# Last output projection: the final column group's weights loaded and split during the three groups ahead of it, and the residuals' loads re-timed

## The chip, the cores and the metric

One core of a Trainium2 chip. The time is device microseconds (us) of one execution of the whole program. Three runs of the kernel before give a median of 988.8 us (988.37 to 990.36).

## The reference, cut to what matters

Two layers of a decoder trunk on one sequence of 256 tokens, model width 2048, all float32. Each layer mixes the tokens (layer 0 a gated linear recurrence, layer 1 sparse attention), gates the result with `silu(z)`, projects it with a 2048 x 2048 matrix and normalises:

```python
h = x
for i in range(DEPTH):                       # DEPTH = 2
    y = mixer_i(h, ...)                      # ... @ w_out at its end
    h = _layer_norm(DEEPNORM_ALPHA * h + y, ln_g, ln_b)
return h
```

The change touches the end of layer 1 alone: `y = (o * silu(z)) @ l1_w_out`, the residual `alpha * h + y` (where `h` is layer 0's output) and the last layer norm.

## The kernel before, in words

**Arithmetic.** A float32 product is made from three matmuls: both operands are split into a high part (rounded by ScalarE, L82) and a low part (the rest, a subtraction on VectorE, L83). `split` (L80-83) does both. For a weight block the low part reads the block and its high part, so it runs after the high part; the block's raw buffer is free when the low part is done.

**The last projection.** `oT` (tiles named `b`, four of them, each four K tiles of 128) holds the gated attention output, transposed and split. The projection runs in four column groups of 512 (`for c in range(4)`, L980). A group's weights come in eight blocks, j = 0 to 7, of 256 rows by 512 columns (512 KB): `load` (L114) issues the DMA on SyncE's queue (SP), `parts` splits it. Groups 0, 1 and 2 use `project` (L173): block by block, both token tiles (t = 0, 1), two K tiles, three matmuls each (L166, L167, L168): 12 matmuls for a block. Blocks 6 and 7 of group 0 need the last tile of `b`, which the last head group of the attention writes at its end (`o` times `zT` on L906, then a split into `b`), first for t = 0, then for t = 1. The matmuls of the groups and those of the attention are interleaved on TensorE by the scheduler, and the order so made is fixed: every engine, and SP's queue, goes through its own list in order.

**Group 3** is done token tile by token tile (`project_by_tile`, L182), so that the layer norm of the first tile runs beside the second's matmuls. It needs all its eight blocks before its first tile ends. `summed` (L964) splits a block into its own tiles (`wh`, `wl` of the pool `late`, eight each) and also adds up the last 256 columns of the block (a reduction on VectorE, L972, and an accumulating copy on ScalarE, L973), from which the second tile's mean is had early.

**Buffers.** `slot` (L149) hands out raw buffers `wr` (three in this stage) and split buffers `wh` and `wl` (five each); whichever is free first is given. In the kernel before, the first three blocks of group 3 use `wr`, the other five are loaded into freed `wh` and `wl` buffers. The pool `late` is opened after group 1 is written down (L1035); its memory is that which the attention's pools (`kv`, `at`) held until `attention.close()`.

**Residuals.** For each group, `h` is rebuilt from layer 0's normalised rows: 512 KB of `norm0`, plus that group's 512 gains and 512 biases spread over the partitions (256 KB each), into a tile of `room`; then GpSimd (POOL) multiplies by the gain (L961, two instructions) and adds the bias (L962, two). When a residual's three loads are issued is written by hand: `turns` (L926) gives for each item n and step i the place (c, j), that is, behind block j of group c. `also` runs at each place, `other` does the step. Items 0 to 3 are the residuals of groups 0 to 3, item 4 the rows of the last norm's gain and bias. A residual with its projection's result gives a piece of `hb` and its statistics (L990, L992, VectorE). Residuals 0 and 2 share a tile of `room`, 1 and 3 another.

Of the kernel before, what the change touches and what calls it, by code (L numbers as in the profile page):

```python
# [8 lines left out]
F32 = mybir.dt.float32  # L9
# [8 lines left out]
D = 2048  # L18
S = 256
NT = S // 128  # L20
KT = D // 128
# [34 lines left out]
def trunk(ctx, tc, a, out):  # L56
# [54 lines left out]

    queued = [None]

    def load(w, j, c0, n, name="wr"):  # L114

        raw = (slot([128, 2, n], F32, name, 3, 1) if name == "wr" else
               slot([128, 1152], F32, name, 5, 3)[:, 0:2 * n].rearrange("p (k n) -> p k n", k=2))
        queued[0] = nc.sync.dma_start(raw, w[256 * j:256 * (j + 1), c0:c0 + n].rearrange(
            "(k p) n -> p k n", p=128)).ins
        return raw  # L120

    def weights(w, j, c0, n):
        return parts(load(w, j, c0, n))
# [55 lines left out]
                also(j)  # L179
        return ps  # L180

    def project_by_tile(xs, w, c0, after, behind=None, summed=None, also=None):  # L182

        ws = []
        for j in range(KT // 2):
            if summed:

                ws.append(summed(load(w, j, c0, 512, "wr" if j < 3 else ("wl", "wh")[j % 2])))
            else:
                hi, lo = weights(w, j, c0, 512)
                ws.append([(hi[:, kk], lo[:, kk]) for kk in range(2)])
            if also:
                also(j)

        def steps(ps, t, i, behind=None):
            for k in range(KT):
                hi, lo = ws[k // 2][k % 2][i:i + 2]  # L200
                with tc.issue_after(behind) if behind and k >= HOLD else nullcontext():
                    tok_step(ps, xs, k, t, hi, lo)
            return ps

        for t in range(NT):
            if summed and t == NT - 1:
                after(t, steps(pjb([128, 258]), t, 2), steps(pjb([128, 256]), t, 4))
            else:
                behind = after(t, steps(pjb([128, 512]), t, 0, behind))
        return behind  # L210
# [179 lines left out]
    with tc.tile_pool(name="start", bufs=4) as start:  # L390
# [3 lines left out]
        ps = mxb([128, 128])  # L394
# [504 lines left out]
    def gate(g, os):  # L899
# [9 lines left out]
        for t in range(NT):  # L909
# [13 lines left out]

    turns = [((0, 6), (0, 7), (0, 7)), ((1, 1), (1, 2), (1, 3)), ((1, 5), (1, 6), (1, 7)),  # L926
             ((2, 1), (2, 2), (2, 3)), ((3, 7), (3, 7), (3, 7), (3, 7))]
    turns = [(n, i, at) for n, v in enumerate(turns) for i, at in enumerate(v)]
    res = {}
    room = [acts.tile([128, 2, 2, 512], F32, name="room", tag="a") for _ in range(4)]  # L930
    rows = [room[i // 2][:, i % 2].rearrange("p u n -> p (u n)") for i in range(4)]
# [7 lines left out]
    def behind(o, src):  # L939
        with tc.issue_after(queued[0]):  # L940
            nc.sync.dma_start(o, src)

    def also(c, j):
        for n, i, at in turns:
            if at == (c, j):
                other(n, i)

    def other(n, i):
        if n == 4:
            i = 2 * (i % 2) + i // 2  # L950
            behind(rows[i], a[("l1_ln_g", "l1_ln_b")[i // 2]][None, D // 2 * (i % 2):D // 2 * (i % 2 + 1)]
                   .to_broadcast([128, D // 2]))
# [2 lines left out]
            behind(res[n][0], norm0[:, 512 * n:512 * (n + 1)].rearrange("(t p) d -> p t d", p=128))  # L955
        else:
            xr, gb = res[n]
            behind(gb[:, i - 1], a[("l0_ln_g", "l0_ln_b")[i - 1]][None, 512 * n:512 * (n + 1)]
                   .to_broadcast([128, 512]))
            for t in range(NT) if i == 2 else ():  # L960
                pool.tensor_tensor(xr[:, t], xr[:, t], gb[:, 0], op=OP.mult)  # L961
# [20 lines left out]
    for c in range(4):  # L982
# [22 lines left out]
        def finish(t, ps, other=None):  # L1005
# [13 lines left out]
            with tc.manual_schedule(engines={mybir.EngineType.DVE}):  # L1019
# [8 lines left out]
                centred(t, me[:, 5:6], (1536, known), (known, D))  # L1028
                scaled(t, mv[:, 3:4], (0, 256), (256, 512), *quarters[1:3], (1536, known), (known, D))

        if c < 3:
            for t, ps in enumerate(project(oT, a["l1_w_out"], 512 * c, lambda j, c=c: also(c, j))):
                residual(t, ps)
            if c == 1:
                late = ctx.enter_context(tc.tile_pool(name="late", bufs=8, side="right"))  # L1035
        else:
            project_by_tile(oT, a["l1_w_out"], 512 * c, finish, summed=summed, also=lambda j: also(3, j))


# [31 lines left out]
```

## Time and profile before

| | us |
|---|---|
| median of three runs | 988.8 |
| the profiled execution, its own time | 989.94 |
| its span, first to last instruction | 987.9 |
| TensorE busy (PE) | 972.9 |
| VectorE busy (DVE) | 695.9 |
| ScalarE busy (ACT) | 564.8 |
| GpSimd busy (POOL) | 111.0 |
| mean granted TensorE clock | 0.995 |

Rows of the profile's timeline give the start in us, the duration, the engine, the line, the operation, output and inputs by their tiles' names, shapes and a count; what stands in brackets is the idle time of the engine just before, and what ended it. `PE` is TensorE's matmuls, `SPq` SyncE's queue of DMA issues. Matmuls are pipelined: the time one costs is the distance to the next one's start, not its duration. A table of windows gives for each stretch the length, the busy time of each engine (with a count of instructions), the granted clock, the DMA engines' share and GB/s.

### The profile page before, as it was taken

What the parts mean: (1) busy time and instruction counts of PE and PEld (TensorE: products, weight loads), DVE (VectorE), ACT (ScalarE), POOL (GpSimd) and SP (SyncE); (2) the same over time, 40 slices, a digit from 0 to 9 for tenths busy, and PEclk for the clock granted to TensorE, in tenths of its full rate; (3) what the DMA queues carried; (4) which work ended last, traced back from release to release, by engine and by line L of the source; (5) the groups of instructions that cost most, each with busy time, mean ns of one, the idle gap of its engine ahead of it and who ended that gap; (6) DMA issues with size and microseconds to landing.
All of it is one profiled execution on the core that took longest, in us unless ns stands there. A gap on an engine that the chain in (4) does not pass through costs nothing.

```text
span 987.9 us, 14450 instructions
## 1 busy us (share of the span) xinstructions
PE 972.9 (98%) x5209; PEld 837.1 (85%) x5209; DVE 695.9 (70%) x1185; ACT 564.8 (57%) x940; POOL 111.0 (11%) x180
## 2 busy tenths in 40 slices
PE   9999999999999999999999999999999999999996
PEld 8888888888888888888888888988888888887885
DVE  6797678657865786656666755655767858797767
ACT  6754554464446544434476655565967747894450
POOL 1400200020002000310010020102001020004320
PEclk9999999999999999999999999999999999999998
DMA  9875565556555655457466776676454555156782
GB/s 306 263 230 176 176 173 168 171 160 192 171 171 161 190 167 171 163 182 259 154 232 209 259 235 207 179 207 182 135 162 138 169 163 140 56 169 213 250 295 94
DMA packets 126247, 185.16 MB, mean 187 GB/s; under 512 B 6224, under 2 KB 70816, under 8 KB 125920
## 3 DMA queue, kind: packets, MB, share of 16 engines
q1 hardware_dynamic: 123984, 177.89, 58.5%
q0 software_dynamic: 1472, 5.56, 1.9%
q8 instruction: 41, 0.67, 0.3%
q10 hardware_dynamic: 720, 0.79, 0.2%
q14 instruction: 30, 0.25, 0.1%
HBM read 180.02 MB, written 4.19 MB: 186 GB/s over the span
## 4 chain that ended last, share of the span: by engine, by line
PE 91%; ACT 3%; DVE 2%; issue 2%; DMA 2%; POOL 0%; SPq 0%; POOLq 0%; DVEq 0%; ACTq 0%
PE pjb L166 18%; PE pjb L168 18%; PE pjb L167 18%; PE pjb L230 13%; PE pjb L234 6%; PE pjb L224 4%; PE pjb L225 2%; PE mxb L506 2%; PE mxb L273 1%; PE mxb L641 1%; PE mxb L642 1%; PE mxb L643 1%; ACT p L848 1%; PE mxb L692 1%; PE mxb L691 1%
## 5 line engine op out<-in xcount | busy, mean ns | idle before, releaser
L83 DVE TENSOR_TENSOR wl<-wr,wh 128x1024 fp32r<-128x1024 f32 (+3 forms) x304 | 365.1, 1208 | 157.1 <-ACT wh L82 155.6
L82 ACT ACTIVATE wh<-wr 128x1024 fp32r<-128x1024 f32 (+3 forms) x304 | 312.1, 1033 | 276.9 <-PE pjb L168 142.8
L167 PE MATMUL pjb<-wl,a 128*128 128x512 f32 (+1 forms) x576 | 219.9, 382 | 0.0
L166 PE MATMUL pjb<-wh,a 128*128 128x512 f32 (+1 forms) x576 | 219.8, 382 | 0.0
L168 PE MATMUL pjb<-wh,a 128*128 128x512 f32 (+1 forms) x576 | 219.3, 381 | 0.0
L230 PE MATMUL pjb<-a,wh 128*128 128x512 f32 x544 | 141.5, 396 | 0.6 <-ACT wh L82 0.4
L168 PEld LDWEIGHTS pjb<-wh,a 128*128 128x128 f32 x576 | 108.4, 188 | 19.2
L166 PEld LDWEIGHTS pjb<-wh,a 128*128 128x128 f32 x576 | 108.2, 188 | 19.2
L167 PEld LDWEIGHTS pjb<-wl,a 128*128 128x128 f32 x576 | 108.3, 188 | 18.6
L230 PEld LDWEIGHTS pjb<-a,wh 128*128 128x128 f32 x544 | 97.3, 189 | 17.9 <-ACT wh L82 1.0
L166 PE MATMUL pjb<-wh,b 128*128 128x512 f32 (+2 forms) x272 | 103.5, 381 | 0.0
L168 PE MATMUL pjb<-wh,b 128*128 128x512 f32 (+2 forms) x272 | 103.5, 380 | 0.0
L167 PE MATMUL pjb<-wl,b 128*128 128x512 f32 (+2 forms) x272 | 103.3, 380 | 0.0
L224 PE MATMUL pjb<-a,wh 128*128 128x512 f32 x256 | 91.2, 396 | 0.0
L234 PEld LDWEIGHTS pjb<-a,wl 128*128 128x128 f32 x544 | 75.9, 188 | 6.3
L234 PE MATMUL pjb<-a,wl 128*128 128x256 f32 x544 | 79.5, 283 | 0.0
L225 PE MATMUL pjb<-a,wl 128*128 128x256 f32 x256 | 72.3, 283 | 0.0
L168 PEld LDWEIGHTS pjb<-wh,b 128*128 128x128 f32 x272 | 51.6, 190 | 9.7
L167 PEld LDWEIGHTS pjb<-wl,b 128*128 128x128 f32 x272 | 51.4, 189 | 9.5
L166 PEld LDWEIGHTS pjb<-wh,b 128*128 128x128 f32 x272 | 51.5, 189 | 9.4
L224 PEld LDWEIGHTS pjb<-a,wh 128*128 128x128 f32 x256 | 48.1, 188 | 10.2
L225 PEld LDWEIGHTS pjb<-a,wl 128*128 128x128 f32 x256 | 48.3, 189 | 0.4
(255 smaller groups left out, 1175.7 us busy)
## 6 DMA issues: line engine op xcount, KB each, us to landing
wr<-in_l_w_in_dram SPq DMA_DIRECT2D x216, 512.0 KB, 3.8
wr<-in_l_w_out_dram SPq DMA_DIRECT2D x59, 512.0 KB, 4.1
ws<-in_l_w_in_dram SPq DMA_DIRECT2D x12, 512.0 KB, 4.6
wr<-in_l_cmp_w_k_dram SPq DMA_DIRECT2D x5, 512.0 KB, 3.5
wr<-in_l_cmp_w_v_dram SPq DMA_DIRECT2D x5, 512.0 KB, 4.1
wr<-in_l_w_in_dram SPq DMA_DIRECT2D x9, 280.0 KB, 3.5
xr<-in_x_dram POOLq DMA_DIRECT2D x4, 512.0 KB, 5.8
norm<-hb POOLq DMA_DIRECT2D x2, 1024.0 KB, 5.6
```

Source lines behind the costliest of these rows:

```text
L82: act.activation(hi, src, AF.Copy)
L83: dve.tensor_tensor(lo, src, hi.bitcast(F32), op=OP.subtract)
L166: pe.matmul(ps, xh, wh, start=(k == 0), stop=False)
L167: pe.matmul(ps, xh, wl, start=False, stop=False)
L168: pe.matmul(ps, xl, wh, start=False, stop=(k == KT - 1))
L224: pe.matmul(ps[b], hi[:, 0, b], xs.both(k), start=(k == 0), stop=False, skip_group_check=True)
L225: pe.matmul(ps[b][:, S:2 * S], lo[:, 0, b], xs.at(k, slice(0, S))[0], start=False, stop=(k == KT - 1), skip_group_check=True)
L230: pe.matmul(o, hi[:, i, b], xs.both(k + i), start=(k + i == 0), stop=False, skip_group_check=True)
L234: pe.matmul(o[:, S:2 * S], lo[:, i, b], xs.at(k + i, slice(0, S))[0], start=False, stop=(k + i == KT - 1), skip_group_check=True)
L273: last[0] = pe.transpose(ps[:, i], src[:, i], ident).ins
L506: pe.matmul(ps[:, h], km[:, h].rearrange("p b r j -> p (b r j)"), later, start=True, stop=True)
L641: pe.matmul(o, a[0], b[0], start=start, stop=False)
```

## The change

Group 3's eight blocks are no longer loaded inside `project_by_tile`. They are item 5 of `turns`: behind certain blocks of groups 0, 1 and 2 `other` loads one, into a raw buffer `wr` like all the others, and hands it to `summed`; the results are kept in `ahead` and passed to `project_by_tile`. The pool `late` is opened ahead of group 0 instead of behind group 1. The loads of the residuals are re-timed; of the two rows of a residual the bias comes second and the gain last, and POOL's work follows the gain. Group 0's residual is written down in group 1, behind block 2 (`residuals(*done)` in `also`), the others as before behind their own group.

| item | before | after |
|---|---|---|
| residual 0 (norm0, then the two rows) | (0,6) (0,7) (0,7) | (0,2) (0,4) (1,0) |
| residual 1 | (1,1) (1,2) (1,3) | (0,6) (1,2) (1,4) |
| residual 2 | (1,5) (1,6) (1,7) | (1,7) (2,0) (2,1) |
| residual 3 | (2,1) (2,2) (2,3) | (2,6) (2,7) (2,7) |
| rows of the last norm | (3,7) | (2,7) |
| group 3's blocks 0 to 7 | in group 3 | (0,5) (0,7) (1,1) (1,3) (1,5) (1,7) (2,1) (2,3) |

```diff
-    def load(w, j, c0, n, name="wr"):
-        raw = (slot([128, 2, n], F32, name, 3, 1) if name == "wr" else
-               slot([128, 1152], F32, name, 5, 3)[:, 0:2 * n].rearrange("p (k n) -> p k n", k=2))
+    def load(w, j, c0, n):
+        raw = slot([128, 2, n], F32, "wr", 3, 1)
...
-    def project_by_tile(xs, w, c0, after, behind=None, summed=None, also=None):
-        ws = []
-        for j in range(KT // 2):
-            if summed:
-                ws.append(summed(load(w, j, c0, 512, "wr" if j < 3 else ("wl", "wh")[j % 2])))
...
+    def project_by_tile(xs, w, c0, after, behind=None, summed=None):
+        ws = summed or []
+        for j in range(KT // 2) if not summed else ():
+            hi, lo = weights(w, j, c0, 512)
...
+    late = ctx.enter_context(tc.tile_pool(name="late", bufs=8, side="right"))
...
+        if (c, j) == (1, 2):
+            residuals(*done)
     def other(n, i):
-        if n == 4:
+        if n == 5:
+            ahead.append(summed(load(a["l1_w_out"], i, D - 512, 512)))
+        elif n == 4:
...
-            behind(gb[:, i - 1], a[("l0_ln_g", "l0_ln_b")[i - 1]][None, 512 * n:512 * (n + 1)]
+            behind(gb[:, 2 - i], a[("l0_ln_b", "l0_ln_g")[i - 1]][None, 512 * n:512 * (n + 1)]
...
         if c < 3:
-            for t, ps in enumerate(project(oT, a["l1_w_out"], 512 * c, lambda j, c=c: also(c, j))):
-                residual(t, ps)
-            if c == 1:
-                late = ctx.enter_context(tc.tile_pool(name="late", bufs=8, side="right"))
+            done = residual, project(oT, a["l1_w_out"], 512 * c, lambda j, c=c: also(c, j))
+            if c:
+                residuals(*done)
         else:
-            project_by_tile(oT, a["l1_w_out"], 512 * c, finish, summed=summed, also=lambda j: also(3, j))
+            project_by_tile(oT, a["l1_w_out"], 512 * c, finish, summed=ahead)
```

In the order rows below a row is the line, the operation, output and inputs, and the shape; the number behind a tile's name tells its instances apart, and line numbers of the kernel after are seven lower to two higher than those of the same statement before.

**SyncE's queue, from the seventh load of group 0's weights.** Before:

```order
L118 DMA wr_8686<-in_l1_w_out_dram 128x2x512
L941 DMA room_8574<-norm0_76 128x2x512
L118 DMA wr_8705<-in_l1_w_out_dram 128x2x512
L941 DMA room_8574<-in_l0_ln_g_dram 128x512
L941 DMA room_8574<-in_l0_ln_b_dram 128x512
L118 DMA wr_8739<-in_l1_w_out_dram 128x2x512
L118 DMA wr_8757<-in_l1_w_out_dram 128x2x512
L941 DMA room_8575<-norm0_76 128x2x512
L118 DMA wr_8776<-in_l1_w_out_dram 128x2x512
```

After (`wr_8691`, `wr_8740` and `wr_8795` are group 3's blocks 0, 1 and 2; `wr_8703` and `wr_8722` blocks 6 and 7 of group 0; `wr_8754`, `wr_8777`, `wr_8807` and `wr_8834` blocks 0 to 3 of group 1):

```order
L117 DMA wr_8691<-in_l1_w_out_dram 128x2x512
L117 DMA wr_8703<-in_l1_w_out_dram 128x2x512
L938 DMA room_8578<-norm0_76 128x2x512
L117 DMA wr_8722<-in_l1_w_out_dram 128x2x512
L117 DMA wr_8740<-in_l1_w_out_dram 128x2x512
L117 DMA wr_8754<-in_l1_w_out_dram 128x2x512
L938 DMA room_8577<-in_l0_ln_g_dram 128x512
L117 DMA wr_8777<-in_l1_w_out_dram 128x2x512
L117 DMA wr_8795<-in_l1_w_out_dram 128x2x512
L117 DMA wr_8807<-in_l1_w_out_dram 128x2x512
L938 DMA room_8578<-in_l0_ln_b_dram 128x512
L117 DMA wr_8834<-in_l1_w_out_dram 128x2x512
```

Three blocks of group 3 stand among the loads of groups 0 and 1, and residual 0's gain now stands behind the first block of group 1. With three raw buffers, each load waits for the block three places ahead in its buffer: `wr_8691` and `wr_8807` share one, `wr_8740` and `wr_8834` the second, and `wr_8722`, `wr_8754`, `wr_8777`, `wr_8795` the third.

**VectorE, from the attention's last gating (`o` times `zT`) on.** Before:

```order
L83 TENSOR_TENSOR wl_8779<-wr_8776,wh_8778 128x1024
L906 TENSOR_TENSOR o_8163<-o_8163,zT_8455 128x256
L906 TENSOR_TENSOR o_8163<-o_8163,zT_8553 128x256
L83 TENSOR_TENSOR b_4571<-o_8163,b_4571 128x4x128
L990 SCALAR_TENSOR_TENSOR hb_8570<-room_8574,pjb_8576 128x256 x2
L992 BN_STATS stats_8571<-hb_8570 128x6 x2
L83 TENSOR_TENSOR wl_8798<-wr_8795,wh_8797 128x1024
L83 TENSOR_TENSOR wl_8821<-wr_8818,wh_8820 128x1024
```

After:

```order
L83 TENSOR_TENSOR wl_8780<-wr_8777,wh_8779 128x1024
L899 TENSOR_TENSOR o_8163<-o_8163,zT_8455 128x256
L899 TENSOR_TENSOR o_8163<-o_8163,zT_8553 128x256
L83 TENSOR_TENSOR b_4571<-o_8163,b_4571 128x4x128
L974 TENSOR_REDUCE ws_8695<-wr_8691 128x1
L974 TENSOR_REDUCE ws_8744<-wr_8740 128x1
L992 SCALAR_TENSOR_TENSOR hb_8570<-room_8577,pjb_8579 128x256 x2
L83 TENSOR_TENSOR wl_8694<-wr_8691,wh_8693 128x2x2x256
L994 BN_STATS stats_8571<-hb_8570 128x6 x2
L83 TENSOR_TENSOR wl_8743<-wr_8740,wh_8742 128x2x2x256
L83 TENSOR_TENSOR wl_8798<-wr_8795,wh_8797 128x2x2x256
```

Before, three blocks of group 1 are split ahead of the last gating (`wl_8779` is the third) and the fourth follows it; after, two are, and what follows the gating is the split of group 3's blocks 0, 1 and 2.

**TensorE, from the last matmuls of group 0's second token tile on.** Before:

```order
L166 MATMUL pjb_8577<-wh_8707,b_4571 128x512
L167 MATMUL pjb_8577<-wl_8708,b_4571 128x512
L168 MATMUL pjb_8577<-wh_8707,b_4571 128x512
L167 MATMUL pjb_8737<-wl_8779,b_4569 128x512
L168 MATMUL pjb_8737<-wh_8778,b_4569 128x512
L166 MATMUL pjb_8738<-wh_8778,b_4569 128x512
```

After:

```order
L165 MATMUL pjb_8580<-wh_8724,b_4571 128x512
L166 MATMUL pjb_8580<-wl_8725,b_4571 128x512
L167 MATMUL pjb_8580<-wh_8724,b_4571 128x512
L165 MATMUL pjb_8752<-wh_8809,b_4569 128x512
L165 MATMUL pjb_8753<-wh_8809,b_4569 128x512
L166 MATMUL pjb_8752<-wl_8810,b_4569 128x512
L167 MATMUL pjb_8752<-wh_8809,b_4569 128x512
```

Both go on to group 1's third block; before, its parts are `wh_8778` and `wl_8779`, after they are `wh_8809` and `wl_8810`, made from `wr_8807`.

## What was predicted ahead of the run

> **What bounds the kernel now.** I read the page first, then a table of windows over the last projection, then who TensorE waited for, then the timelines of TensorE, VectorE, ScalarE, GpSimd and the DMA queue around the one gap. The page's second line says who bounds:
>
> ```profile
> PE 972.9 (98%) x5209; PEld 837.1 (85%) x5209; DVE 695.9 (70%) x1185; ACT 564.8 (57%) x940; POOL 111.0 (11%) x180
> ```
>
> The windows show where TensorE, in this stage, isn't busy (second figure) or not at full clock (0.97, 0.86):
>
> ```profile
> 890.00:900.00 10.00, 7.57 (x38) 5.72 (x37) 7.73 (x7) 5.30 (x9) 5.83 (x4) 0.97 0.98 312
> 900.00:910.00 10.00, 10.00 (x39) 8.06 (x38) 7.67 (x8) 3.32 (x4) 6.06 (x4) 0.86 0.49 160
> 910.00:920.00 10.00, 10.00 (x46) 8.29 (x45) 6.42 (x11) 4.62 (x5) 0.00 (x0) 1.00 0.52 148
> ...
> 950.00:960.00 10.00, 10.00 (x45) 8.23 (x44) 8.33 (x17) 6.66 (x15) 0.00 (x0) 1.00 1.01 352
> ```
>
> From 898 us on, the list of TensorE's waits has one entry, this gap; here it is with what follows:
>
> ```profile
> 895.30 0.40 PE L167 MATMUL pjb<-wl,b 128*128 128x512 f32 x1
> 898.02 0.50 PE L641 MATMUL mxb<-pt,vals 128*128 128x512 f32 x1 [2.33 <-DVE pt L83]
> ...
> 899.95 0.63 PE L643 MATMUL mxb<-pt,vals 128*128 128x512 f32 x1
> ...
> 902.91 0.39 PE L168 MATMUL pjb<-wh,b 128*128 128x512 f32 x1
> ...
> 910.07 0.39 PE L166 MATMUL pjb<-wh,b 128*128 128x512 f32 x1
> ...
> 912.79 0.39 PE L166 MATMUL pjb<-wh,b 128*128 128x512 f32 x1
> ...
> 978.09 0.28 PE L168 MATMUL pjb<-wh,b 128*128 128x256 f32 x1
> ```
>
> 2.33 us idle; then seven matmuls take 2.96 us (899.95 to 902.91) where at full clock twelve take 2.72 (910.07 to 912.79, 0.227 each): 2.96 - 1.59 = 1.4 us more. The stage loses 3.7 us in all. From 903 to 978.4 TensorE goes without a break, so no load or split of the last group is waited for now. Behind the last matmul lie the last norm's VectorE work and the output, 9.5 us to the span's end, which no edit alters: what TensorE's end moves, the time moves.
>
> Why the gap: VectorE's rows, one from ScalarE, one from GpSimd, one from SyncE's queue.
>
> ```profile
> 852.74 0.76 DVE L906 TENSOR_TENSOR o<-o,zT 128x256 f32<-128x256 f32 x2 [0.78 <-ACT zT L903]
> ...
> 893.31 1.23 DVE L83 TENSOR_TENSOR wl<-wr,wh 128x1024 fp32r<-128x1024 f32 x1 [2.27 <-ACT wh L82]
> 894.45 2.91 DVE L906 TENSOR_TENSOR o<-o,zT 128x256 f32<-128x256 f32 x2
> 897.29 1.28 DVE L83 TENSOR_TENSOR pt<-mxb,pt 128x512 fp32r<-128x512 f32 x2
> ...
> 903.42 2.01 DVE L83 TENSOR_TENSOR wl<-wr,wh 128x1024 fp32r<-128x1024 f32 x1 [0.79 <-ACT wh L82]
> ```
>
> ```profile
> 892.22 1.06 ACT L82 ACTIVATE wh<-wr 128x1024 fp32r<-128x1024 f32 x1 [1.86 <-DMA wr<-in_l_w_out_dram]
> ```
>
> ```profile
> 893.90 3.18 POOL L961 TENSOR_TENSOR room<-room 128x512 f32<-128x512 f32 x2 [73.28 <-DMA room<-in_l_ln_g_dram]
> 897.04 2.69 POOL L962 TENSOR_TENSOR room<-room 128x512 f32<-128x512 f32 x2
> ```
>
> ```profile
> 888.36 0.37 SPq L118 DMA_DIRECT2D wr<-in_l_w_out_dram  x1
> ```
>
> A load issued at 888.36 lands at 892.2 (3.9 us); its high part, its low part, then the attention's gating `o` times `zT`, and the low part of `pt` for which TensorE waits. The gating takes 2.91 us where it takes 0.76 alone: GpSimd works on residual 0 just then, 5.9 us in its two rows.
>
> **What goes.** Residual 0's gain is now issued behind group 1's first block, so GpSimd is quiet at 894.5. The wait for the load stays, with the seventh block in the place of the eighth. The gating ends 2.91 - 0.76 = 2.15 us earlier, the gap shrinks to 0.2, and I take the slow clock to go with it (1.4): **-3.5 us**. If a gap of 0.2 still cost clock, it would be -2.1.
>
> Here the Trainium skill (TensorE: Matmul & The Clock Gate, Part 1: The HAM clock gate) says that the clock halves after an idle window of about 3.4 us. By it alone a gap of 2.33 us need not have cost the 1.4, and the sum below would be 1.4 us higher; the trace shows the slow matmuls right behind this gap, so it decides.
>
> **What comes first: two raw buffers held through the attention's end.** Group 3's blocks 0 and 1 are loaded early (`wr_8691` in the place of `wr_8686`, `wr_8740` after 894.5), but their split is only in VectorE's list behind the attention's last write into `b`: their tiles lie in memory that the attention's keys and values hold till then. So two of three raw buffers are held, and `wr_8722`, `wr_8754`, `wr_8777` follow each other through the third. Costs used, besides those above:
>
> ```profile
> 908.84 1.32 DVE L906 TENSOR_TENSOR o<-o,zT 128x256 f32<-128x256 f32 x2 [0.45 <-ACT o L890]
> 910.92 0.69 DVE L83 TENSOR_TENSOR b<-o,b 128x512 fp32r<-128x512 f32 x1 [0.76 <-ACT b L82]
> 912.16 0.75 DVE L990 SCALAR_TENSOR_TENSOR hb<-room,pjb 128x256 f32<-128x256 f32 x2 [0.55 <-DVE b L83]
> ...
> 950.59 0.41 DVE L972 TENSOR_REDUCE ws<-wr 128x1 f32<-128x256 f32 x1
> ```
>
> ```profile
> 910.25 0.63 ACT L82 ACTIVATE b<-o 128x512 fp32r<-128x512 f32 x1 [1.45 <-DVE o L906]
> ```
>
> In the old trace's clock (a low part follows the next at 1.15): 894.5 seventh block split; 895.2 gating; 896.5 two `pt` parts; 897.7 eighth block split, its buffer goes to block 0 of group 1 (`wr_8754`). +3.9 landed, +1.06 high, +2.01 low (GpSimd works on residual 0 now): 904.7, block 1 (`wr_8777`) issued. +3.9, +1.06, +1.15: 910.8. Gating 0.76, high part of `b` 0.63, low 0.69: 912.9. Two reductions (0.7), a residual pair (0.75), low part of group 3's block 0 (1.15): 915.5. Only now is block 2 of group 1 (`wr_8807`) issued: landed 919.4, high part 920.5, low 921.7.
>
> TensorE meanwhile, started at 895.9: it waits 0.2 and 0.7 for the two parts of the last `pt` (queued behind block 0's parts in ScalarE's and VectorE's lists) and about 1.3 for block 1's two parts: **+2.2**. Ten matmuls from 910.8 and the twelve of group 0's second tile end at 915.8; the next needs block 2's high part: idle till 920.5, two matmuls, 0.8 more for the low part: **+5.5**. A gap of 4.7 us costs the slow clock anew, at least as the 2.33 did: **+1.4**. Bounds of these 9.1: the fastest landing (3.7, row below), GpSimd not in the way, no slow clock: 5.8; all three landings at the median of 5.0: 12.4.
>
> **What comes next: a ring of two.** From block 2 of group 1 the group's blocks alternate between two raw buffers; the third goes from one block of group 3 to the next.
>
> ```profile
> DMA to landing us min/median/max: 3.7/5.0/7.3
> ```
>
> ```profile
> L83 DVE TENSOR_TENSOR wl<-wr,wh 128x1024 fp32r<-128x1024 f32 x19 | 27.3, 1445 | 11.9 <-ACT wh L82 11.7
> L82 ACT ACTIVATE wh<-wr 128x1024 fp32r<-128x1024 f32 x18 | 19.1, 1061 | 26.1 <-DMA wr<-in_l_w_out_dram 19.3 <-PE pjb L168 6.7
> ```
>
> The first line is of the loads between 885 and 955, the other two of the splits from 900 to 966. One turn is landing, high, low: 5.0 + 1.06 + 1.22 = 7.3 us, and it brings two blocks, which TensorE eats in 24 x 0.227 = 5.4. Before, three buffers brought three blocks (8.2 us of matmuls) in the same turn, with room to spare. Three turns follow in which TensorE has nothing else: 3 x 1.9 = 5.6 us. The slow clock of the first stall covers 1.4 of it, and at each turn two matmuls run on the high part while the low is made (3 x 0.45). **+2.8**. Bounds: 0 (turn of 3.9 + 2.3 = 6.2, covered) to 6 (splits at the mean of 1.45, landing 5.5). From group 2's second block on, TensorE's list holds 22 matmuls of group 3's first tile between the blocks, 5.0 us, which covers the remaining three turns.
>
> The same transfers move in both; the added adding-up is the same too, only earlier. What remains is costed at nothing: the last residual's late loads (some 10 us of matmuls of group 3 cover them; uncovered, GpSimd's 6 us would show ahead of the last norm).
>
> **Sum:** -3.5 + 2.2 + 5.5 + 1.4 + 2.8 = +8.4. On the profiled execution: 989.94 + 8.4 = 998.3; that execution lies 1.1 us above the median, so against the median 988.8 + 8.4 = **997.2 us**.
>
> A second rule weighs against this size. The Trainium skill (DMA: Bandwidth & Descriptors, Anatomy of one DMA) gives 2.0 us plus bytes at 436 GB/s, measured on another issue path: 512 KB would land in an estimated 3.2 us. The ring's turn would then be 5.5 us, as long as the matmuls, and the three landings of the first stall 2.1 shorter: +3.5 in place of +8.4. No row lands that fast (least 3.7); the rival below takes the same side from rows.
>
> **The rivals.** *Only the first stall* (chance 0.22): the ring keeps up, landings near 3.9 since fewer transfers are in flight at once. Then +8.4 - 2.8 = 5.6, or less with 3.7 and GpSimd out of the way: 5.8 - 3.5 = 2.3; middle 4: 992.8. For: 3.9 at 888.36; against: the median.
>
> *Faster* (0.08): the held buffers don't matter, because TensorE comes later to block 2 than I reckon or group 3's first split runs early. It decides at one point: block 2's high part must be there by 915.8, so its issue must come by 910.8 in place of 915.5. ScalarE idle 26.1 us in that stretch speaks for it; the place of that split in VectorE's list against. Then only the gain remains: 988.8 - 3.5 = 985.3.
>
> *Worse* (0.09): landings of 5.5 to 6 with three transfers and residuals in flight, each low part slowed by GpSimd, and the slow clock at every turn: 12.4 - 3.5 + 6 = +15: 1003.7.
>
> *Balance* (0.05): stall and gain cancel, 987 to 990.8.
>
> **How the numbers follow.** The forecast's own case has 0.56 (994.5 to 1001). The range, 991.5 to 1003, takes in *Only the first stall* and half of *Worse*. A measurement of this kernel can tell about 0.2% (2 us) from no change. Faster by more: 0.08. Within: 0.06 (*Balance* and the lowest end of the first rival). Slower: 0.86.
>
> **What would show it.** Right: the gating pair at 0.76 us and a gap under 0.5 us in its place; a TensorE wait of 4 to 6 us, ended by ScalarE's high part, on the first matmul of group 1's third block; slow clock behind it; then waits of 1 to 2 us at every second block till group 2's start, and none in group 3. Wrong: VectorE splitting group 3's first block ahead of the attention's end, or TensorE full from 905 to 978.

## The result and the profile after

| | before | after |
|---|---|---|
| median of four runs each, us | 988.59 | 1000.58 |
| the profiled execution, its own time | 989.94 | 1000.56 |
| its span | 987.9 | 998.8 |
| start of TensorE's last matmul in it | 978.09 | 989.09 |

The ratio is 1.012, with a 95% interval of 1.0102 to 1.0137: 12.0 us slower. The forecast was 997.2, slower by 8.4. The sign was right and the time within the range; the size was 3.6 us short, and the experiments show that this is not one small error but four, of both signs.

Who TensorE waited for from 880 us to the end, in the kernel after (us in total, times, the longest):

```profile
PE pjb L165 <- ACT wh L82: 5.7, 4, 4.4
PE pjb L166 <- DVE wl L83: 2.4, 3, 1.3
PE mxb L635 <- DVE pt L83: 0.6, 1, 0.6
PE mxb L634 <- DVE pt L83: 0.2, 1, 0.2
```

Before, one gap of 2.33 us stood here. It is gone; 8.9 us in nine waits have come, all but the last two lines on the parts of a weight block. Windows of the kernel after, in the columns of the prediction's:

```profile
910.00:920.00 10.00, 5.31 (x23) 4.05 (x22) 8.78 (x19) 5.49 (x11) 0.00 (x0) 0.90 0.48 142
920.00:930.00 10.00, 8.78 (x26) 6.00 (x26) 5.55 (x8) 4.61 (x11) 1.33 (x2) 0.76 0.79 267
930.00:940.00 10.00, 8.92 (x32) 7.21 (x33) 8.37 (x7) 4.75 (x7) 6.61 (x3) 0.83 0.71 232
940.00:950.00 10.00, 9.12 (x39) 6.83 (x38) 8.61 (x16) 5.39 (x10) 3.81 (x3) 1.00 0.74 256
950.00:960.00 10.00, 10.00 (x45) 8.18 (x44) 8.06 (x8) 4.80 (x8) 4.20 (x2) 1.00 0.73 237
```

The counts behind PE say more than its busy time: 23, 26 and 32 matmuls in the first three windows where 45 fit in the last, and the clock at 0.76 and 0.83 in two of the windows. VectorE's busy times, 8.78 and 8.37 of 10 us, are high but not full. TensorE's rows that wait, and the slow ones behind them:

```profile
895.50 0.50 PE L634 MATMUL mxb<-pt,vals 128*128 128x512 f32 x1 [0.16 <-DVE pt L83]
...
905.12 0.50 PE L635 MATMUL mxb<-pt,vals 128*128 128x512 f32 x1 [0.61 <-DVE pt L83]
...
909.28 0.73 PE L165 MATMUL pjb<-wh,b 128*128 128x512 f32 x2 [0.21 <-ACT wh L82]
910.54 0.50 PE L166 MATMUL pjb<-wl,b 128*128 128x512 f32 x1 [0.52 <-DVE wl L83]
...
920.19 1.22 PE L165 MATMUL pjb<-wh,b 128*128 128x512 f32 x2 [4.36 <-ACT wh L82]
...
924.61 0.48 PE L165 MATMUL pjb<-wh,b 128*128 128x512 f32 x1
...
929.04 0.73 PE L165 MATMUL pjb<-wh,b 128*128 128x512 f32 x2 [0.76 <-ACT wh L82]
931.08 0.50 PE L166 MATMUL pjb<-wl,b 128*128 128x512 f32 x1 [1.31 <-DVE wl L83]
...
931.67 0.63 PE L166 MATMUL pjb<-wl,b 128*128 128x512 f32 x1
...
935.06 0.63 PE L165 MATMUL pjb<-wh,b 128*128 128x512 f32 x2
...
943.76 0.73 PE L165 MATMUL pjb<-wh,b 128*128 128x512 f32 x2 [0.35 <-ACT wh L82]
945.02 0.50 PE L166 MATMUL pjb<-wl,b 128*128 128x512 f32 x1 [0.53 <-DVE wl L83]
...
989.09 0.28 PE L167 MATMUL pjb<-wh,b 128*128 128x256 f32 x1
```

The long wait stands where the prediction put it, on the first matmul of group 1's third block. From 920.19 to 924.61 nine matmuls take 4.42 us where they would take 2.04 at 0.227 each: 2.4 us more. Some 1.8 of it is slow clock (0.43 each, 922.05 to 924.61); the rest is mostly a pause for the low part, done at 921.4. From 931.67 to 935.06 eight take 3.39 instead of 1.82: 1.6 us. VectorE on the way to the long wait, then ScalarE's two high parts on it:

```profile
894.10 0.75 DVE L899 TENSOR_TENSOR o<-o,zT 128x256 f32<-128x256 f32 x2
...
911.91 0.69 DVE L83 TENSOR_TENSOR b<-o,b 128x512 fp32r<-128x512 f32 x1 [0.76 <-ACT b L82]
912.70 0.75 DVE L974 TENSOR_REDUCE ws<-wr 128x1 f32<-128x256 f32 x2
914.02 1.22 DVE L83 TENSOR_TENSOR wl<-wr,wh 128x1024 fp32r<-128x1024 f32 x1
...
920.17 1.23 DVE L83 TENSOR_TENSOR wl<-wr,wh 128x1024 fp32r<-128x1024 f32 x1 [0.54 <-ACT wh L82]
...
929.02 4.23 DVE L83 TENSOR_TENSOR wl<-wr,wh 128x1024 fp32r<-128x1024 f32 x2 [1.63 <-ACT wh L82]
```

```profile
912.64 1.06 ACT L82 ACTIVATE wh<-wr 128x1024 fp32r<-128x1024 f32 x1 [0.76 <-DVE b L83]
...
919.08 1.06 ACT L82 ACTIVATE wh<-wr 128x1024 fp32r<-128x1024 f32 x1 [2.50 <-DMA wr<-in_l_w_out_dram]
```

The first row is the gating, back at 0.75. ScalarE takes group 3's first block up at 912.64, released not by its landing but by the attention's last write into `b`. The low part of that block (914.02) ends at 915.2; only then is its raw buffer free for group 1's third block, whose low part is done at 921.4. In the prediction's chain these ends were 915.5 and 921.7. VectorE's last row is a pair of splits of 2.1 us each, beside GpSimd's residual 1 (928.67 to 936.6). What the loads between 885 and 955 us took to land, and the splits of 900 to 966 us:

```profile
DMA to landing us min/median/max: 3.6/4.6/6.4
```

```profile
L83 DVE TENSOR_TENSOR wl<-wr,wh 128x1024 fp32r<-128x1024 f32 x23 | 33.1, 1443 | 19.9 <-ACT wh L82 19.7
L82 ACT ACTIVATE wh<-wr 128x1024 fp32r<-128x1024 f32 x23 | 24.3, 1059 | 35.1 <-DMA wr<-in_l_w_out_dram 34.3 <-DVE b L83 0.8
```

The loads land no later than before (median 4.6 against 5.0), yet ScalarE waits 34.3 us for them instead of 19.3 (20.7 with the five blocks that were then loaded into `wh` and `wl`): they are issued later, not slower.

### The profile page after: what moved, and what is told of

Same layout as the page of the kernel before. It is cut to its first block, busy times and chain, and to the rows that moved or that the text cites. A ratio compares the mean times of both kernels' runs of the same rounds, so it can differ in the third digit from the quotient of the medians.

```text
span 998.8 us, 14445 instructions
## 1 busy us (share of the span) xinstructions
PE 978.0 (98%) x5209; PEld 837.9 (84%) x5209; DVE 694.8 (70%) x1185; ACT 564.7 (57%) x940; POOL 113.1 (11%) x180
## 4 chain that ended last, share of the span: by engine, by line
PE 87%; DMA 4%; ACT 3%; DVE 3%; issue 2%; POOL 0%; POOLq 0%; DVEq 0%; ACTq 0%
PE pjb L166 17%; PE pjb L167 17%; PE pjb L165 17%; PE pjb L223 13%; PE pjb L227 6%; PE pjb L217 4%; DMA wr<-in_l_w_out_dram 4%; PE pjb L218 2%; PE mxb L499 2%; DVE wl L83 1%; PE mxb L266 1%; ACT wh L82 1%; PE mxb L634 1%; PE mxb L635 1%; ACT p L841 1%
## 5 line engine op out<-in xcount | busy, mean ns | idle before, releaser
L83 DVE TENSOR_TENSOR wl<-wr,wh 128x1024 fp32r<-128x1024 f32 (+3 forms) x309 | 371.8, 1209 | 169.0 <-ACT wh L82 167.9
L82 ACT ACTIVATE wh<-wr 128x1024 fp32r<-128x1024 f32 (+3 forms) x309 | 317.5, 1033 | 289.3 <-PE pjb L167 131.4
L167 PEld LDWEIGHTS pjb<-wh,a 128*128 128x128 f32 x576 | 108.3, 188 | 19.3
L165 PEld LDWEIGHTS pjb<-wh,a 128*128 128x128 f32 x576 | 108.2, 188 | 19.3
L223 PEld LDWEIGHTS pjb<-a,wh 128*128 128x128 f32 x544 | 97.4, 189 | 16.9
```

The lines of the kernel that those rows point to most:

```text
L82: act.activation(hi, src, AF.Copy)
L83: dve.tensor_tensor(lo, src, hi.bitcast(F32), op=OP.subtract)
L165: pe.matmul(ps, xh, wh, start=(k == 0), stop=False)
L167: pe.matmul(ps, xl, wh, start=False, stop=(k == KT - 1))
L223: pe.matmul(o, hi[:, i, b], xs.both(k + i), start=(k + i == 0), stop=False, skip_group_check=True)
```

## The experiments

**Theory.** Two prices of raw buffers (held through the attention's end; a ring of two behind it) make the loss, and the gap's 3.5 us are a gain that the buffers hide. **Rivals.** The residuals' new place costs; or the splits as such are too much for the engines in groups 1 and 2.

Whole times differ by 1 or 2 us from run to run, so beside each ratio stands a length read from the profiled execution: from the end of TensorE's work ahead of the attention's `vals` matmul at 895 to 898 us (its start less its wait) to the start of the last matmul. Before: 898.02 - 2.33 = 895.69 to 978.09, 82.4 us; after: 895.34 to 989.09, 93.8 us.

| kernel | that length | ratio to before, 95% interval |
|---|---|---|
| after | 93.8 | 1.0120 (1.0102 to 1.0137) |
| ahead loads, residuals as before | 94.4 | 1.0127 (1.0106 to 1.0149) |
| own buffers for two blocks | 88.4 | 1.0050 (1.0032 to 1.0067) |
| own buffers for all | 82.8 | 1.0013 (1.0001 to 1.0025) |
| own buffers, from group 1 on | 82.4 | 1.0002 (0.9993 to 1.0011) |
| own buffers, residuals 1 to 3 as before | 83.9 | 1.0017 (1.0004 to 1.0029) |
| first block ahead in group 1 | 88.2 | 1.0053 (1.0034 to 1.0072) |
| one block ahead in group 0 | 92.8 | 1.0088 (1.0073 to 1.0102) |
| three blocks ahead in group 0 | 97.4 | 1.0151 (1.0131 to 1.0170) |
| before, all residuals later | 83.6 | 1.0013 (1.0002 to 1.0025) |
| before, residual 0 alone later | 81.1 | 0.9981 (0.9972 to 0.9990) |
| the same, four blocks ahead | 80.0 | 0.9981 (0.9969 to 0.9992) |
| the same, two blocks ahead | 82.5 | 1.0001 (0.9990 to 1.0011) |

**The two halves apart.** First the residuals alone, on the kernel before:

```diff
-    turns = [((0, 6), (0, 7), (0, 7)), ((1, 1), (1, 2), (1, 3)), ((1, 5), (1, 6), (1, 7)),
-             ((2, 1), (2, 2), (2, 3)), ((3, 7), (3, 7), (3, 7), (3, 7))]
+    turns = [((0, 2), (0, 4), (1, 0)), ((0, 6), (1, 2), (1, 4)), ((1, 7), (2, 0), (2, 1)),
+             ((2, 6), (2, 7), (2, 7)), ((3, 7), (3, 7), (3, 7), (3, 7))]
...
+        if (c, j) == (1, 2):
+            residuals(*done)
...
+            behind(gb[:, 2 - i], a[("l0_ln_b", "l0_ln_g")[i - 1]][None, 512 * n:512 * (n + 1)]
...
```

> The kernel before with the second half of the change alone: the residuals' table and the swapped scale, group 0's residual one group later; group 3's weights are loaded and split in group 3 as before. Buffers theory: this half is the gain that the prediction counted (3.5 us: the gating's pair back from 2.91 to 0.76, the gap of 2.33 us before the first output matmul and the 1.4 us of half clock behind it gone), so 988.6 - 3.5 = 985.1 us, range 984 to 987. Rival, the residuals' new place is what costs (GpSimd's work beside the splits of groups 1 and 2, where the changed kernel's split pair took 4.23 us): 990 to 995 us.

It came out slower, at 1.0013 and 990.92 us: the theory failed here, and the time lies in the rival's range. TensorE, VectorE and GpSimd of this kernel:

```profile
895.59 0.50 PE L641 MATMUL mxb<-pt,vals 128*128 128x512 f32 x1 [0.17 <-DVE pt L83]
...
950.66 0.50 PE L167 MATMUL pjb<-wl,b 128*128 128x512 f32 x1 [1.42 <-DVE wl L83]
```

```profile
948.71 4.13 DVE L83 TENSOR_TENSOR wl<-wr,wh 128x1024 fp32r<-128x1024 f32 x2
...
957.04 0.41 DVE L974 TENSOR_REDUCE ws<-wh 128x1 f32<-128x256 f32 x1
...
957.48 1.23 DVE L83 TENSOR_TENSOR wl<-wh 128x1024 fp32r<-128x1024 f32 x1
958.62 0.41 DVE L974 TENSOR_REDUCE ws<-wl 128x1 f32<-128x256 f32 x1
```

```profile
946.98 2.54 POOL L963 TENSOR_TENSOR room<-room 128x512 f32<-128x512 f32 x2 [11.78 <-DMA room<-in_l_ln_g_dram]
949.48 4.50 POOL L964 TENSOR_TENSOR room<-room 128x512 f32<-128x512 f32 x2
```

The gap went as forecast. But residual 3 now stands beside group 3's first splits, which take 2.07 us each, and TensorE waits 1.42 us. Behind that a second limit shows. A block of group 3 costs VectorE about 1.6 us from one reduction to the next (957.04 to 958.62), more where other work falls between, and its first token tile six matmuls, 1.36 us: in this pass VectorE's splits set the pace, and a TensorE that comes sooner catches up with them.

Then the loads alone, on the kernel after, with the residuals' table, the order of the rows and the writing down as before:

```diff
-    turns = [((0, 2), (0, 4), (1, 0)), ((0, 6), (1, 2), (1, 4)), ((1, 7), (2, 0), (2, 1)),
-             ((2, 6), (2, 7), (2, 7)), ((2, 7), (2, 7), (2, 7), (2, 7)),
+    turns = [((0, 6), (0, 7), (0, 7)), ((1, 1), (1, 2), (1, 3)), ((1, 5), (1, 6), (1, 7)),
+             ((2, 1), (2, 2), (2, 3)), ((2, 7), (2, 7), (2, 7), (2, 7)),
...
```

> The changed kernel with the first half alone: group 3's weights ahead, the residuals where they were before. Buffers theory: the loss without the gain, 1000.6 + 3.5 = 1004.1 us, range 1001.5 to 1006. TensorE's first wait on ScalarE's high part stays at 4 to 6 us and the gap of 2 us before the first output matmul is back. Rival, the residuals' new place costs: 994 to 998 us.

1002.52 us, where 1004.1 was expected; the interval overlaps that of the kernel after. The long wait is there (4.75 us at 920.77), the gap is not:

```profile
895.48 0.50 PE L634 MATMUL mxb<-pt,vals 128*128 128x512 f32 x1 [0.16 <-DVE pt L83]
```

GpSimd starts residual 0 only at 895.55 us in this kernel, 1.65 us later than before and past the gating, which takes 0.76 us at 894.07. So the gap does not need the residuals' new table to close; here it closed without it, and what the table adds to the loads ahead is not more than the two intervals hide.

**Own buffers.** The two `room` tiles for the last norm's rows lie idle until block 7 of group 2; their four halves serve as raw buffers. For the first two blocks:

```diff
-            ahead.append(summed(load(a["l1_w_out"], i, D - 512, 512)))
+            if i < 2:
+                raw = room[0][:, i]
+                behind(raw, a["l1_w_out"][256 * i:256 * (i + 1), D - 512:D].rearrange("(k p) n -> p k n", p=128))
+            else:
+                raw = load(a["l1_w_out"], i, D - 512, 512)
+            ahead.append(summed(raw))
```

> The changed kernel with buffers of their own (two idle room halves) for the first two blocks ahead alone; the other six go through the three raw buffers as in the changed kernel. It parts the two prices that the prediction named: the buffers held through the attention's end, and the ring that eight more blocks turn through. Buffers theory: the wait of 4.36 us, the small ones ahead of it (0.61 + 0.21 + 0.52) and the half clock behind it go, the later waits (0.76 + 1.31 + 0.35 + 0.53 and their half clock, some 5 us) stay: between the 1000.6 of the changed kernel and the 991.2 of own buffers for all, 994.5 us, range 992.5 to 996.5. Rival, VectorE's row of splits behind the attention's end makes the wait as long without a shortage of buffers: 998 us and above.

994.72 us, 0.2 from the expectation. The 4.36 us at 920.19 are gone; what is left is the ring:

```profile
924.30 1.22 PE L165 MATMUL pjb<-wh,b 128*128 128x512 f32 x2 [3.15 <-ACT wh L82]
...
940.53 0.97 PE L165 MATMUL pjb<-wh,b 128*128 128x512 f32 x3 [1.69 <-ACT wh L82]
```

The code is otherwise that of the kernel after, and the splits of the two blocks still stand behind the attention's end (912.11 and 913.91). So the held buffers are what cost 1.0120 - 1.0050, 6.9 us. The size is less sure than the cause: the profiled execution of this kernel, 996.76 us, is its slowest, and by the lengths in the table the price is 93.8 - 88.4 = 5.4. For all eight blocks:

```diff
-            ahead.append(summed(load(a["l1_w_out"], i, D - 512, 512)))
+            raw = room[i // 2 % 2][:, i % 2]
+            behind(raw, a["l1_w_out"][256 * i:256 * (i + 1), D - 512:D].rearrange("(k p) n -> p k n", p=128))
+            ahead.append(summed(raw))
```

> The changed kernel with the blocks ahead landing in the four halves of the two room tiles that lie idle until the last rows are loaded, at the same places of the code; the other groups keep three raw buffers. Loads, splits and residuals are as many as in the changed kernel. Buffers theory: every wait of TensorE behind the attention goes but what the splits queue up themselves (under 1 us), and 985.1 us come out, range 984 to 989. Rival, the splits and loads as such are too much for groups 1 and 2: 995 us and above, with the waits on ScalarE's high part and VectorE's low part still there.

The ring's price is 1.0050 - 1.0013, another 3.7 us (5.6 by the lengths): with both buffer prices gone, 10.6 of the 12.0 us are. But 985.1 was expected and 991.15 came, no faster than before. TensorE and VectorE:

```profile
919.26 0.50 PE L166 MATMUL pjb<-wl,b 128*128 128x512 f32 x1 [1.68 <-DVE wl L83]
```

```profile
910.21 2.25 DVE L83 TENSOR_TENSOR wl<-room,wh 128x1024 fp32r<-128x1024 f32 x1
912.38 0.74 DVE L996 BATCH_NORM_STATS2 stats<-hb 128x6 f32<-128x256 f32 x2
913.05 5.03 DVE L83 TENSOR_TENSOR wl<-room,wh 128x1024 fp32r<-128x1024 f32 x3
918.00 1.21 DVE L83 TENSOR_TENSOR wl<-wr,wh 128x1024 fp32r<-128x1024 f32 x1
```

The waits are now on VectorE's low part: four splits of group 3 stand ahead of the one that TensorE needs, the first at 2.25 us beside GpSimd. TensorE's later waits are of 0.5 us each. Here the rival of the splits themselves holds in place, if not in size (995 and above): with the buffers out of the way, they cost what the gap had brought. Two attempts to spread them. From block 1 of group 1 on:

```diff
-             ((0, 5), (0, 7), (1, 1), (1, 3), (1, 5), (1, 7), (2, 1), (2, 3))]
+             ((1, 1), (1, 2), (1, 3), (1, 5), (1, 7), (2, 1), (2, 3), (2, 5))]
```

> Blocks ahead in buffers of their own (the idle room halves) and taken from block 1 of group 1 on, none before the attention's end. With own buffers from group 0 on, six splits stood in one row on VectorE from 908.9 to 920.9 us and TensorE waited 1.68 us for one of them, with half clock behind it (37 matmuls in 910 to 920 where 46 fit). Buffers theory with VectorE's burst as the rest: spread out, that wait goes or falls under 0.7 us, and 991.2 - 1.7 - 1.9 = 987.6 us come out, range 985 to 990. Rival, whichever way they are spread the eight extra splits beside GpSimd's residuals cost as much as they save: 990 to 993 us.

989.97 us, ratio 1.0002: the rival's range. Three splits beside GpSimd's residual 1 took 6.13 us, and TensorE waited 2.12. Then apart from it, with the residuals 1 to 3 of the kernel before:

```diff
...
-             ((0, 5), (0, 7), (1, 1), (1, 3), (1, 5), (1, 7), (2, 1), (2, 3))]
+             ((1, 4), (1, 6), (2, 0), (2, 1), (2, 2), (2, 3), (2, 4), (2, 5))]
```

> All eight blocks ahead in buffers of their own, from block 4 of group 1 on (4, 6, then 0 to 5 of group 2), with the residuals of groups 1 to 3 at the places of the kernel before. With own buffers from block 1 of group 1 on, GpSimd's residual 1 (909.6 to 918.4 us) stood beside three blocks' splits in a row (6.13 us on VectorE for the three) and TensorE waited 2.12 us, 35 matmuls in 910 to 920 us where 45 fit. Theory: apart from each other both go their way, the wait falls under 0.8 us and 985 to 986 us come out, ratio 0.9955, range 0.9935 to 0.9985. Rival, six blocks more in group 2 alone are too much for one queue and VectorE: waits of 1 to 2 us there and a ratio of 1.000 to 1.004.

1.0017: again the rival, with waits for low parts of 1.52 us at 937.72 and 2.38 us at 951.34. Both stand beside GpSimd's residuals again (928.65 to 936.5 and 944.73 to 952.4), so the splits were not kept apart from them. In none of the three places did eight more splits go into groups 1 and 2 for nothing.

**How many blocks are held.** Three runs moved the first blocks, without own buffers.

```diff
-             ((0, 5), (0, 7), (1, 1), (1, 3), (1, 5), (1, 7), (2, 1), (2, 3))]
+             ((1, 1), (1, 2), (1, 3), (1, 5), (1, 7), (2, 1), (2, 3), (2, 5))]
```

> The changed kernel with the first two blocks ahead taken in group 1 (blocks 1, 2, 3, 5, 7 of group 1 and 1, 3, 5 of group 2 instead of 5 and 7 of group 0 on), so that no raw buffer is held through the attention's end. Buffers theory: the wait of 4.36 us and the small ones ahead of it (0.16 + 0.61 + 0.21 + 0.52) go, and the half clock behind them (26 matmuls in 10 us where 45 fit, some 3 us of it); of the later waits (0.76 + 1.31 + 0.35 + 0.53 and their half clock) most stay, since eight more blocks still turn through three buffers within two groups: 1000.6 - 5.9 - 3 = 991.7 us, range 988 to 995. Rival, the engines' work in groups 1 and 2 is the bound (16 blocks' splits in the time of 16 blocks' matmuls and not the buffers): the waits only move and 997 to 1001 us come out.

```diff
+             ((0, 7), (1, 1), (1, 2), (1, 3), (1, 5), (1, 7), (2, 1), (2, 3))]
```

> The changed kernel with one block ahead instead of two taken before the attention's end (block 7 of group 0, then 1, 2, 3, 5, 7 of group 1 and 1, 3 of group 2). Buffers theory: one raw buffer held leaves two in turn, and while one block turns in 7.3 us (5.0 to land, 1.06 and 1.22 to split) another lies ready, so the wait of 4.36 us shrinks to 0 to 1.5 us: 995 us, range 992 to 998, near the 995.6 of none held. Rival, any held block costs its share (half of the 5.0 us between none held and two held): 998 us.

```diff
+             ((0, 4), (0, 5), (0, 7), (1, 3), (1, 5), (1, 7), (2, 1), (2, 3))]
```

> The changed kernel with three blocks ahead instead of two taken before the attention's end (blocks 4, 5 and 7 of group 0, then 3, 5, 7 of group 1 and 1, 3 of group 2). Buffers theory: all three raw buffers wait for VectorE's first split behind the attention's last step, at about 914 us, so that the first block of group 1 itself is loaded only then and split by about 921, 15 us behind where the changed kernel had it; TensorE has some 5 us of work less than the changed kernel to cover it with and stands 6 to 12 us longer, with half clock behind it: 1010 us, range 1005 to 1016. Rival, the loss is not the buffers held but the splits' work in groups 1 and 2: as many splits, so 999 to 1002 us.

Measured 995.64, 998.47 and 1005.26 us. The order is as expected, the sizes are not: the first came out 0.6 us above its range, the second where its rival had it, the third 5 us under the forecast at the lower end of its range, with a wait of 5.26 us at 916.49. The runs don't count what they were meant to count. With none taken in group 0, two group 3 blocks' sums and splits still stand behind the attention's last write into `b`:

```profile
908.27 0.69 DVE L83 TENSOR_TENSOR b<-o,b 128x512 fp32r<-128x512 f32 x1 [0.76 <-ACT b L82]
909.41 0.74 DVE L974 TENSOR_REDUCE ws<-wr 128x1 f32<-128x256 f32 x2 [0.44 <-DVE b L83]
910.73 1.22 DVE L83 TENSOR_TENSOR wl<-wr,wh 128x1024 fp32r<-128x1024 f32 x1
```

Their loads had gone out from group 1's blocks ahead of the attention's end all the same, as the loads run ahead of the matmuls. What these runs show is only that holding earlier costs more; the price itself is from the own buffers.

**What of the gap's gain can be kept.** On the kernel before, residual 0 alone later, the others in their places (with the order of a residual's two rows and the writing down of group 0 as in the change):

```diff
-    turns = [((0, 6), (0, 7), (0, 7)), ((1, 1), (1, 2), (1, 3)), ((1, 5), (1, 6), (1, 7)),
+    turns = [((0, 2), (0, 4), (1, 0)), ((1, 1), (1, 2), (1, 3)), ((1, 5), (1, 6), (1, 7)),
...
```

> The kernel before with group 0's residual alone one group later and its scale last; the residuals of groups 1 to 3 stay where they were. With all of them later, the gap of 2.33 us before the first output matmul went (46 matmuls in 890 to 900 us instead of 38, 45 instead of 39 in the next 10) and as much was lost where GpSimd's work on residual 3 (947 to 954 us) now met group 3's first splits: a pair of them took 4.13 us, TensorE waited 1.42 us and 35 matmuls ran in 950 to 960 where 44 had. Theory: residual 3 back in its place, the gain of 3.2 to 3.5 us stays: 989.2 - 3.4 = 985.8 us on this chip's scale, ratio 0.9966, range 0.9950 to 0.9985. Rival, the gap's 3.4 us are covered by something else that then ends last: ratio 1.000 or above.

0.9981: 1.9 us faster, the interval clear of 1, but half of what was expected. TensorE:

```profile
896.13 0.50 PE L641 MATMUL mxb<-pt,vals 128*128 128x512 f32 x1 [0.17 <-DVE pt L83]
...
960.24 0.50 PE L167 MATMUL pjb<-wl,b 128*128 128x512 f32 x1 [0.77 <-DVE wl L83]
964.49 0.50 PE L167 MATMUL pjb<-wl,b 128*128 128x512 f32 x1 [0.80 <-DVE wl L83]
...
977.07 0.28 PE L168 MATMUL pjb<-wh,b 128*128 128x256 f32 x1
```

Nothing waits between, and then group 3 takes part of it back. With half of group 3 ahead in own buffers, the last idea for a better version:

```diff
+             ((1, 4), (1, 6), (2, 1), (2, 3))]
...
+            if summed and j < len(ahead):
+                ws.append(ahead[j])
+            elif summed:
+                ws.append(summed(load(w, j, c0, 512, "wr" if j < 7 else "wl")))
```

> The kernel before with group 0's residual one group later (as in the run with that alone, ratio 0.9981) and four of group 3's eight blocks ahead, landing in the idle room halves, at blocks 4 and 6 of group 1 and 1 and 3 of group 2; the other four are loaded in group 3 through the raw buffers. In the run with the residual alone TensorE waited 0.77 and 0.80 us for group 3's fifth and sixth block's low parts on VectorE, with half clock behind them, and its last matmul came only 1 us earlier than in the kernel before though 16 more matmuls had run by 910 us. Theory: with four blocks split ahead these waits go and the whole of the gap's price stays: 989.9 - 1.9 - 2.5 = 985.5 us, ratio 0.9955, range 0.993 to 0.9975. Rival, the extra splits in groups 1 and 2 meet GpSimd's residuals and TensorE waits there as much: ratio 0.998 to 1.002.

0.9981 again, against the 0.9955 expected. The number is in the rival's range, but its mechanism is not what the trace has: group 3's waits are gone, one of 0.62 us at 943.21 is left, and the measured length is the shortest of all, 80.0. In the whole time the two kernels can't be told apart. And with two blocks ahead, where of the six others the last three go into freed `wh` and `wl` buffers:

```diff
-             ((1, 4), (1, 6), (2, 1), (2, 3))]
+             ((1, 4), (1, 6))]
...
-                ws.append(summed(load(w, j, c0, 512, "wr" if j < 7 else "wl")))
+                ws.append(summed(load(w, j, c0, 512, "wr" if j < 5 else ("wl", "wh")[j % 2])))
```

> As the kernel with four of group 3's blocks ahead in the idle room halves (ratio 0.9981, one wait of 0.62 us in group 2 where the third and fourth block's splits stood, and 42 matmuls in 940 to 950 us where 46 fit), but with the first two blocks alone, at blocks 4 and 6 of group 1, where nothing waited. Theory: group 2 runs without a wait; group 3's loads end two blocks sooner than with the residual alone, so of its waits of 0.77 and 0.80 us one at most is left: from the gap on (896 us) to the last matmul 79.0 to 80.3 us, against 80.2 with four ahead, 81.4 with none and 82.7 before; ratio 0.9970, range 0.9955 to 0.9985. Rival, group 3's own splits set its end: 81 us and more, and a ratio of 0.998 to 1.000.

1.0001, a miss; the rival's group 3 it was:

```profile
949.62 0.51 PE L166 MATMUL pjb<-wh,b 128*128 128x512 f32 x1 [0.57 <-ACT wh L82]
951.29 0.50 PE L167 MATMUL pjb<-wl,b 128*128 128x512 f32 x1 [1.16 <-DVE wl L83]
```

Group 3's first block of its own is late here (ScalarE waited 4.61 us for its landing, till 947.16), and the slow clock follows the two waits: eight matmuls whose starts lie 0.43 us apart. With the residual alone it had waited 4.16 us, till 944.05. Why that load comes later with two blocks ahead wasn't tried.

## Why the prediction was right, and where it was not

By its steps, with what each measured (differences of ratios, times 989 us; each is uncertain by some 2 us):

| step | forecast, us | shown, us |
|---|---|---|
| what goes: gating and gap | -3.5 | in its place -3.6; 1.9 faster by itself, in the run with residual 0 alone later |
| two raw buffers held | +9.1 | +6.9: own buffers for two (5.4 by the lengths) |
| a ring of two | +2.8 | +3.7: own buffers for all, less the former (5.6 by the lengths) |
| the splits, "only earlier" | 0 | +4.8: what is left of own buffers for all (+1.3, where -3.5 was expected); 4.0 by the lengths |
| sum | +8.4 | -3.5 + 6.9 + 3.7 + 4.8 = +11.9 |

**What goes.** The gating is back at 0.75, the gap at 0.16, no slow matmul stands behind it: -2.2 - 1.4 = -3.6, as forecast. But it is no gain of the whole: in the kernel before, a TensorE that comes sooner catches up with group 3's splits, so the gap was partly slack. That loading the last group ahead could lift just this limit is not borne out by any whole time: the best of them (four blocks ahead) has no wait in group 3 left, but is no faster than the residual alone.

**Two raw buffers held.** The mechanism held link by link: the split of group 3's first block behind the attention's end, the buffer that waits for it, the landing, the two parts, each end within 0.4 us of the chain. The size was mis-taken both ways: 4.36 where 5.5 stood, 0.61 + 0.21 + 0.52 where 2.2 did, and 2.4 behind the long wait, some 1.8 of it slow clock, where 1.4 did.

**A ring of two.** Its waits, 0.76 + 1.31 + 0.35 + 0.53 = 2.95 us, come to the 2.8 forecast, and none lies in group 3. That the sums agree is partly luck: three stalls were forecast, at every second block, and two came, at group 1's fifth block (929.04 and 931.08) and at group 2's first (943.76 and 945.02). Not in the sum was that they would slow the clock once more (1.6 us). Nor were the landings to blame: their median was lower than before. The Trainium skill (DMA: Bandwidth & Descriptors, Anatomy of one DMA) had them at an estimated 3.2 us. None of this trace was under 3.6. The ring stalled though the landings were quicker than the 5.0 assumed, with a pair of low parts at 2.1 us each beside GpSimd where 1.22 had been reckoned.

**The step that failed** is "the added adding-up is the same too, only earlier", costed at nothing, and with it the splits. The cover named for it was no row but the engines' idle time in the stage. The splits come in rows, behind the attention's end and beside GpSimd's residuals, and each row stands ahead of the split that TensorE needs next. The 4.8 us are a remainder, counted from the full gain of 3.5. Set against the kernel with the residuals' table alone (1.0013 as well, lengths 83.6 and 82.8), the eight blocks ahead in buffers of their own cost nothing more: their waits, 1.68 + 0.23 + 0.53 + 0.52 us, stand in the place of group 3's, 1.42 + 0.32 + 0.46 + 0.79. So the remainder holds two things, the splits' new waits and a gain of the residuals that does not last; the runs don't divide it between these, nor between VectorE's list and GpSimd. The other term costed at nothing, the last residual's late loads, did cost nothing: from the last matmul's start to the span's end it is 9.8 us before and 9.7 after.

About 2.3 us of the 11.4 by which the length grows from before to after are in no row: -3.6, 8.7 of waits (8.9 less the 0.16) and 4.0 behind them make 9.1. Each restart costs a little more than its wait (the second matmul behind a wait starts some 0.1 us late), and some pauses are too short for the list; they were not resolved one by one.

## What to carry to other kernels

A block loaded ahead costs its buffer until its consumer can run, and a consumer whose output lies in memory still in use can't run: before loading ahead, look for the write that frees the destination, and give such blocks buffers outside the ring. A gap on the bounding engine is worth its length only if no other engine is close behind in the stages after it; look there for the work that the gap had let catch up. Work moved "earlier" is not free because an engine is idle on the mean: ask which instruction it will stand ahead of, and beside whom.

## What the runs showed of the hardware

**The clock.** How long a pause it takes to slow TensorE does not come out as one length. Before, 2.33 us were enough, and 2.11 were (one block ahead, at 942.15). After 2.12 (own buffers from group 1 on), 2.38 (own buffers, residuals 1 to 3 as before) and 1.68 us (own buffers for all) no matmul was slow, and the granted clock was 1.00 there. So the half clock that two expectations put behind the 1.68 us, and behind the 0.77 and 0.80 us of the residual alone, was not there. Two short pauses close together were enough or were not: 0.76 and 1.31 us, 0.57 and 1.16, and 1.09 and 0.53 (first block ahead in group 1, at 936.99) were; 1.19 and 1.60 us (the same kernel, at 920.88) were not. Behind the pauses under 3 us the slow stretch was 3.0 to 3.4 us long: 899.53 to 902.91 us before, 931.67 to 935.06 after. Behind those of 3.15 us and more it began with the first matmul and lasted 4.4 to some 6.5 us, with what further waits fell into it. The Trainium skill (TensorE: Matmul & The Clock Gate, Part 1: The HAM clock gate) has a free-running window of about 3.4 us and lets the clock fall after an idle window. The length of the short stretches agrees; the idle window does not, since all the pauses ahead of them were shorter. A window that runs freely would let the same pause cost clock or not by when it falls; no run here set that.

**VectorE beside GpSimd.** The split of 128x1024 takes 1.22 us alone and 1.7 to 2.3 beside GpSimd's 128x512 multiplications and additions. The delay does not grow with the operation. In the kernel after, a low part of 128x4 that takes 0.15 us alone takes 1.25 beside residual 1:

```profile
935.38 1.25 DVE L83 TENSOR_TENSOR wl<-ws,wh 128x4 fp32r<-128x4 f32 x1
```

The reduction at 933.17, with one input, stays at 0.41 beside the same residual. The Trainium skill (SBUF — State Buffer, SBUF: two separate sides) has an operation of VectorE with two inputs in SBUF share a port with GpSimd as a lock held for the whole instruction. The rows agree in that the delay is 0.5 to 1.1 us whatever the size, less than one of GpSimd's instructions (1.27 to 2.25 us).
